# Gate and up of a gated feed-forward layer as one 2x2x2 block product with seven half products, with h kept in DRAM

## The chip, the cores and the metric

One core of a Trainium2 chip. The metric is the device time of one execution in microseconds. Engines: TensorE (PE, with its weight load PEld), VectorE (DVE), ScalarE (ACT), GpSimd (POOL), and SyncE (SP), which issues nearly all DMAs.

## The reference, cut to what matters

One hybrid decoder layer in fp32 on 1024 tokens of width 1024; D_FF = 2816. After the two attention groups and their output projection:

```python
x  = layer_norm(alpha * x + (1 + gate_m) * y, ln1_g, ln1_b)
u2 = x * (1 + scale_f) + shift_f
y2 = (silu(u2 @ w_gate) * (u2 @ w_up)) @ w_down
x  = layer_norm(alpha * x + (1 + gate_f) * y2, ln2_g, ln2_b)
```

Names below: z is the normalized row before ln1_g and ln1_b; x1 = z * ln1_g + ln1_b; h = silu(gate) * up.

## The kernel before, in words

Tokens are in two halves of 512, w_gate and w_up in 22 column blocks f of 128, the width 1024 in 8 slices k of 128. Every fp32 product is three TensorE matmuls (`mm3`): each operand is split into a high part, a cast made by ACT, and a low part, `raw - hi`, made by DVE (`split`, lines 87 and 88), and hi·hi, hi·lo and lo·hi are added in PSUM. One matmul has a 128x128 stationary operand and 512 moving columns. All matmuls of the feed-forward are of this kind, apart from the last row block.

The order within each engine is set by the framework's scheduler, which reorders the program text by its own model; what comes out is fixed before the run and each engine goes through its own list strictly in order. So are the DMAs that SP issues.

- `mixer_units(half, ...)` (lines 829 to 858): per 128 token rows and 512 columns, 12 matmuls `yo`; DVE adds (847), POOL multiplies by the gate (848), DVE adds the residual (849) and takes statistics; with the second column half, mean and 1/sqrt follow on DVE and POOL (`ln_scale`, line 796 on POOL), and ACT writes z (856). Half 0 runs inside the attention, half 1 behind it, in the PSUM tiles b3, w0 and w1.
- `make_u2(rt, mi)` (870 to 886): per slice k, four transposes on TensorE (879), one ACT instruction that applies the modulation (881), a split. It gives u2 of one half of the tokens.
- `mixer_affine` (860 to 866): 16 POOL instructions that turn z into x1; x1 of half 1 goes to DRAM (`x1_d`).
- `ffn_up(us)` (892 to 917): per f, load and split the 128 columns of w_gate and of w_up (two DMAs of 512 KB), 2 x 8 x 3 = 48 matmuls into the two banks of one wide PSUM tile, silu on ACT, product and split on DVE and ACT; h stays in SBUF as hi and lo (the slots `HT`).
- `ffn_down` (919 to 979): per half of the tokens and half of the columns, w_down loaded and split in 11 pieces; 528 matmuls per half of the tokens. At the end of the last quarter four pieces are kept back so that row blocks finish one after the other; the last row block is in two parts of 256 columns. Then `out_norm` (981 to 998).

The text's order is half 0's u2, half 1's mixer units, `ffn_up` of half 0, u2 of half 1, down of half 0, up of half 1, down of half 1. Matmuls of the feed-forward: 2 x 22 x 48 = 2112 for gate and up, 2 x 528 = 1056 for down.

Of the kernel before, what the change touches and what calls it, by code (L numbers as in the profile page):

```python
# [33 lines left out]
def hymba_layer_kernel(  # L34
# [767 lines left out]
    x1_d = dp.tile([S // 2, D], F32, name="x1_d")  # L802
# [23 lines left out]

    ybank = [0]

    def mixer_units(half, rt, yt):
# [3 lines left out]
        def unit(h, q, nb):  # L833
# [6 lines left out]
            tag = ("b3",)[0] if nb == 1 else ('b3', 'w0', 'w1')[ybank[0] % 3]  # L840
# [10 lines left out]
            if h == 1:  # L851
# [37 lines left out]
    HT = (4, 5, 6, 7, 24, 25, 34, 35, 10, 11, 12, 13, 26, 27, 28, 29, 30, 31, 36, 37, 14, 15)  # L889
    fc = [0]  # L890

    def ffn_up(us, between=()):
        ht = []
        between = list(between)
        for f2 in range(NF // 2):
            hh = slot(HT[2 * f2], (2, 512), dt=F32R, name="hh")
            hl = slot(HT[2 * f2 + 1], (2, 512), dt=F32R, name="hl")
            for a in range(2):
                f = 2 * f2 + a
                fs = slice(f * P, (f + 1) * P)  # L900
                ps = wide(f"w{fc[0] % 2}", "gu")
                fc[0] += 1
                for m, w in enumerate((w_gate, w_up)):
                    wh, wl = load_split((NK, P), w[:, fs].rearrange("(k p) n -> p k n", p=P))
                    for k in range(NK):
                        mm3(
                            ps[:, m * 512 : (m + 1) * 512], wh[:, k, :], wl[:, k, :], us[k][0], us[k][1],
                            k == 0, k == NK - 1,
                        )
                sg = tmp512("sg")  # L910
                nc.scalar.activation(sg, ps[:, 0:512], AF.Silu)
                nc.vector.tensor_tensor(sg, ps[:, 512:1024], sg, op=ALU.mult)
                split(hh[:, a, :], hl[:, a, :], sg)
# [165 lines left out]
```

## Time and profile before

| | |
|---|---|
| time, median of 3 runs (lowest to highest) | 1359.32 us (1359.19 to 1360.11) |
| span of the profiled execution | 1358.9 us |
| difference of the span to the median | 0.4 us |
| PE busy | 1319.3 us, 97% |
| DVE / ACT / POOL busy | 625.8 / 482.8 / 246.6 us |
| share of PE in the chain that ended last | 85% |
| matmul records (of all parts) | 6671 |

The profiled execution's own time is not listed apart from its span, so sums are made against the span and 0.4 us is what lies around it. To read the page: the share of busy time is an average over stages; what a change in one stage is worth shows in that stage, by what PE waited for there. A matmul's record lasts longer than the distance to the next one, since matmuls overlap, so the cost of one is the distance of starts.

### The profile page before, as it was taken

What the parts mean: (1) busy time and instruction counts of PE and PEld (TensorE: products, weight loads), DVE (VectorE), ACT (ScalarE), POOL (GpSimd) and SP (SyncE); (2) the same over time, 40 slices, a digit from 0 to 9 for tenths busy, and PEclk for the clock granted to TensorE, in tenths of its full rate; (3) what the DMA queues carried; (4) which work ended last, traced back from release to release, by engine and by line L of the source; (5) the groups of instructions that cost most, each with busy time, mean ns of one, the idle gap of its engine ahead of it and who ended that gap; (6) DMA issues with size and microseconds to landing.
All of it is one profiled execution on the core that took longest, in us unless ns stands there. A gap on an engine that the chain in (4) does not pass through costs nothing.

```text
span 1358.9 us, 16771 instructions
## 1 busy us (share of the span) xinstructions
PE 1319.3 (97%) x6671; PEld 1071.2 (79%) x6671; DVE 625.8 (46%) x927; ACT 482.8 (36%) x812; POOL 246.6 (18%) x244
## 2 busy tenths in 40 slices
PE   5999999999999999988999999999999999999997
PEld 4889987898876666666888888888888888888886
DVE  7665556714353566586433333324373333332244
ACT  3423264423455566443233222522122322222121
POOL 3400114400142454349300000000020000000004
PEclk9999999999999999998999999999999999999999
DMA  9865511110022236314533333332373333332221
GB/s 300 252 221 183 173 48 47 24 32 32 17 64 78 56 108 220 140 47 124 155 93 93 94 93 93 114 119 93 94 216 93 94 96 97 100 95 93 93 94 62
DMA packets 155872, 147.43 MB, mean 108 GB/s; under 512 B 6305, under 2 KB 128267, under 8 KB 155793
## 3 DMA queue, kind: packets, MB, share of 16 engines
q1 hardware_dynamic: 155792, 146.35, 35.0%
q8 instruction: 52, 0.85, 0.3%
q14 instruction: 28, 0.22, 0.1%
HBM read 131.50 MB, written 10.50 MB: 105 GB/s over the span
## 4 chain that ended last, share of the span: by engine, by line
PE 85%; DMA 5%; DVE 5%; ACT 2%; POOL 1%; issue 1%; SPq 0%; POOLq 0%; DVEq 0%; ACTq 0%
PE gu L101 12%; PE gu L100 12%; PE gu L99 12%; PE dn L937 6%; PE dn L938 6%; PE dn L939 6%; DMA wc<-in_w_c_dram 4%; PE pv L756 4%; PE tr L746 3%; PE acc L330 2%; PE acc L331 2%; PE acc L332 2%; PE acc L100 2%; PE acc L101 2%; PE acc L99 2%; PE sc L716 1%
## 5 line engine op out<-in xcount | busy, mean ns | idle before, releaser
L88 DVE TENSOR_TENSOR lo<-raw,hi 128x1024 fp32r<-128x1024 f32 (+1 forms) x161 | 208.1, 1293 | 461.6 <-ACT hi L87 461.6
L87 ACT CAST hi<-raw 128x1024 fp32r<-128x1024 f32 (+1 forms) x161 | 168.9, 1050 | 467.4 <-PE gu L100 272.5
L101 PE MATMUL gu<-u2h,lo 128*128 128x512 f32 x704 | 280.6, 399 | 7.4 <-DVE lo L88 7.4
L100 PE MATMUL gu<-u2l,hi 128*128 128x512 f32 x704 | 279.3, 397 | 2.0 <-DVE u2l L88 2.0
L99 PE MATMUL gu<-u2h,hi 128*128 128x512 f32 x704 | 275.5, 392 | 0.0
L101 PEld LDWEIGHTS gu<-u2h,lo 128*128 128x128 f32 x704 | 132.6, 188 | 36.5 <-DVE lo L88 7.8
L100 PEld LDWEIGHTS gu<-u2l,hi 128*128 128x128 f32 x704 | 132.6, 188 | 34.4 <-DVE u2l L88 2.9
L99 PEld LDWEIGHTS gu<-u2h,hi 128*128 128x128 f32 x704 | 134.6, 191 | 31.2
L796 POOL TENSOR_TENSOR mv<-mv,half_neg 128x1 f32<-128x1 f32 x16 | 21.2, 1327 | 674.3 <-DVE mv L795 674.1
L937 PE MATMUL dn<-hi,hh 128*128 128x512 f32 (+1 forms) x334 | 128.9, 386 | 0.0
L938 PE MATMUL dn<-lo,hh 128*128 128x512 f32 (+1 forms) x334 | 128.4, 385 | 0.0
L939 PE MATMUL dn<-hi,hl 128*128 128x512 f32 (+1 forms) x334 | 127.5, 383 | 0.0
L330 PE MATMUL acc<-hi,uh 128*128 128x264 f32 (+1 forms) x384 | 108.7, 284 | 1.3 <-ACT osb L530 0.8
L331 PE MATMUL acc<-lo,uh 128*128 128x264 f32 (+1 forms) x384 | 108.6, 283 | 0.0
L332 PE MATMUL acc<-hi,ul 128*128 128x264 f32 (+1 forms) x384 | 108.6, 283 | 0.0
L330 PEld LDWEIGHTS acc<-hi,uh 128*128 128x128 f32 x384 | 72.7, 190 | 2.5 <-ACT osb L530 1.0
L331 PEld LDWEIGHTS acc<-lo,uh 128*128 128x128 f32 x384 | 72.8, 190 | 0.8 <-issue 0.5
L939 PEld LDWEIGHTS dn<-hi,hl 128*128 128x128 f32 x334 | 62.6, 188 | 13.7
L937 PEld LDWEIGHTS dn<-hi,hh 128*128 128x128 f32 x334 | 62.7, 188 | 13.4
L721 DVE CUSTOM_DVE_ANT_0 pr<-sc,smask 128x128 f32<-128x128 f32 (+7 forms) x64 | 47.9, 754 | 55.0 <-PE sc L717 31.4
L938 PEld LDWEIGHTS dn<-lo,hh 128*128 128x128 f32 x334 | 62.8, 188 | 12.7
L332 PEld LDWEIGHTS acc<-hi,ul 128*128 128x128 f32 x384 | 72.6, 189 | 0.3
(233 smaller groups left out, 2041.2 us busy)
## 6 DMA issues: line engine op xcount, KB each, us to landing
raw<-in_w_gate_dram SPq DMA_DIRECT2D x44, 512.0 KB, 4.0
raw<-in_w_up_dram SPq DMA_DIRECT2D x44, 512.0 KB, 3.8
raw<-in_w_down_dram SPq DMA_DIRECT2D x44, 512.0 KB, 3.7
wc<-in_w_c_dram SPq DMA_DIRECT2D x32, 512.0 KB, 4.5
wc<-in_w_c_dram SPq DMA_DIRECT2D x32, 256.0 KB, 6.7
raw<-in_w_in_dram SPq DMA_DIRECT2D x15, 512.0 KB, 4.0
raw<-in_w_o_dram SPq DMA_DIRECT2D x12, 512.0 KB, 6.3
xb<-in_x_dram SPq DMA_DIRECT2D x8, 512.0 KB, 5.9
```

Source lines behind the costliest of these rows:

```text
L87: nc.scalar.copy(dst_hi, src)
L88: nc.vector.tensor_tensor(dst_lo, src, dst_hi.bitcast(F32), op=ALU.subtract)
L99: nc.tensor.matmul(ps, lh, rh, start=start, stop=False)
L100: nc.tensor.matmul(ps, lh, rl, start=False, stop=False)
L101: nc.tensor.matmul(ps, ll, rh, start=False, stop=stop)
L330: nc.tensor.matmul(ps, uh[k][:, ts], wh[:, k % 4, :], start=k == 0, stop=False)
L331: nc.tensor.matmul(ps, uh[k][:, ts], wl[:, k % 4, :], start=False, stop=False)
L332: nc.tensor.matmul(ps, ul[k][:, ts], wh[:, k % 4, :], start=False, stop=k == NK - 1)
L756: nc.tensor.matmul(pv[64 * par : 64 * par + 64, 0:256], fv_t(kb)[:, 64 * h : 64 * h + 64], pt[:, par, a * 256 : (a + 1) * 256], start=kb == 0,
L937: nc.tensor.matmul(pq, hh[:, qs], wh[:, c0:c1], start=f == 0, stop=False)
L938: nc.tensor.matmul(pq, hh[:, qs], wl[:, c0:c1], start=False, stop=False)
L939: nc.tensor.matmul(pq, hl[:, qs], wh[:, c0:c1], start=False, stop=f == NF - 1)
```

## The change

Gate and up of all 1024 tokens are taken as one product of 2x2 blocks: the width in two halves (k 0 to 3, k 4 to 7), the tokens in two halves, and gate and up of one block f as the two halves of the columns. Instead of eight half products (each four slices of three matmuls, 12 matmuls) seven are made, by Strassen's identity in the form with few additions. A11 and A12 are the width halves of u2 of half 0 of the tokens, A22 that of half 1; S1 to S4 are sums of the A blocks, B11 and B21 are blocks of w_gate, B22 one of w_up, T1 to T4 sums of the B blocks. Per f: 84 matmuls for both halves of the tokens, 96 before. `first_operands` makes A11 and A12 (A blocks of half 0), `second_operands` A22 and S1 to S4 of the whole run once, `sum_weights` T1 to T4 per f, and `group_parts` the products and the sums of their results (`c11` is a wide PSUM tile with P1 and P2 in one bank and P6 in the other; `x_` and `y_` are single banks).

h of all tokens goes to DRAM per f (`h_d`, 22 stores of 512 KB) and comes back, split again, per pair of f and half of the tokens (`load_h`, 22 loads). `ffn_down` takes one half of the tokens with both column halves in all eight PSUM banks; w_down is loaded 2 x 11 x 2 times as before, and three pieces are kept back at the end of each half. The last row block is 512 columns wide. z instead of x1 goes to DRAM (`z_d`, 8 stores), and the 16 POOL instructions of `mixer_affine` stand in `rows_in`, at the beginning of each `ffn_down`. Half 1's mixer units use the banks b2 and b3. w_gate and w_up are loaded once: 44 DMAs, 88 before. `gaT` and `l2b` share a tag.

```diff
-            tag = ("b3",)[0] if nb == 1 else ('b3', 'w0', 'w1')[ybank[0] % 3]
+            tag = UNIT_BANKS[nb][ybank[0] % len(UNIT_BANKS[nb])]
...
                 nc.scalar.activation(r, r, AF.Identity, bias=mv[:, 3:4], scale=mv[:, 2:3])
+                nc.sync.dma_start(z_d[ts, :], r)
...
+    def second_operands(rt):
...
+        for j in range(NJ):
+            for a in range(2):
+                u2_rows(rt, j + NJ * a, xs[j][:, a, :], f"b{a}")
...
+        for j in range(NJ):
+            t = slot(S_HL[j][4], (2, 512), dt=F32R, name="a22")
+            split(t[:, 0, :], t[:, 1, :], xs[j][:, 1, :])
...
+            nc.vector.tensor_tensor(xs[j][:, 1, :], xs[j][:, 0, :], xs[j][:, 1, :], op=ALU.add)
+            nc.vector.tensor_tensor(xs[j][:, 0, :], af[j][:, 0, :], xs[j][:, 0, :], op=ALU.subtract)
...
+            split(hi, lo, xs[j])
...
+        for j in range(NJ):
+            nc.vector.tensor_tensor(af[j][:, 0, :], xs[j][:, 1, :], af[j][:, 0, :], op=ALU.subtract)
+            nc.vector.tensor_tensor(af[j][:, 1, :], af[j][:, 1, :], af[j][:, 0, :], op=ALU.subtract)
...
+            split(hi, lo, af[j])
...
+    def sum_weights(f, g, u, w):
...
+        nc.vector.tensor_tensor(t12[:, 0], u[:, 0:NJ], g[:, 0:NJ], op=ALU.subtract)
+        nc.vector.tensor_tensor(t12[:, 1], u[:, NJ:NK], t12[:, 0], op=ALU.subtract)
+        nc.vector.tensor_tensor(t34[:, 0], u[:, NJ:NK], u[:, 0:NJ], op=ALU.subtract)
+        nc.vector.tensor_tensor(t34[:, 1], g[:, NJ:NK], t12[:, 1], op=ALU.subtract)
...
+        split(h, l, t12)
...
+        split(h, l, t34)
...
+        split(b[:, 0], b[:, 1], u[:, NJ:NK])
...
+        def p12_a():
+            c11 = st_["c11"] = wide(f"w{par}", "gu")
...
+            product(c11[:, 0:512], w["B11"], opnd["A11"], True)
+            nc.scalar.copy(u, c11[:, 0:512])
+        def p12_b():
+            product(st_["c11"][:, 0:512], w["B21"], opnd["A12"], False)
+        def p6():
+            u, c = st_["u"], st_["c11"]
+            product(c[:, 512:1024], w["T2"], opnd["S2"], True)
+            nc.vector.tensor_tensor(u, c[:, 512:1024], u, op=ALU.add)
...
+        def p43():
...
+            product(x_, w["T4"], opnd["A22"], False)
+            nc.vector.tensor_tensor(g[:, 1, :], x_, u, op=ALU.add)
+            product(y_, w["B22"], opnd["S4"], False)
+            nc.vector.tensor_tensor(h[:, 0, :], y_, u, op=ALU.add)
+            nc.scalar.activation(g[:, 0, :], st_["c11"][:, 0:512], AF.Silu)
+            nc.scalar.activation(g[:, 1, :], g[:, 1, :], AF.Silu)
+            nc.vector.tensor_tensor(h, g, h, op=ALU.mult)
+            nc.sync.dma_start(h_d[f // 2][f % 2, :, :], h.rearrange("p a n -> p (a n)"))
...
+        def load_h(i, hi, lo):
+            raw = slot(HRAW[pc[0] % 2], (2, 512), name="hr")
+            nc.sync.dma_start(raw, h_d[i][:, :, half * 512 : (half + 1) * 512].rearrange("f p n -> p f n"))
+            split(hi, lo, raw)
...
+    first_operands(xa)
     for f in mixer_units(1, xb, yb):
-        f(2)
+        f(3)
+    second_operands(xb)
...
+            p12_a()
+            p6()
+            p12_b()
+        p7()
+        p5()
+        mid()
+        p43()
...
+    rows = {0: rows_in(0), 1: None}
...
+    ffn_down(0)
+    rows[1] = rows_in(1)
+    ffn_down(1)
```

PE behind the last `yo` matmuls of half 1's mixer units, before (`gu` with `u2h`, `u2l` are gate and up of half 0):

```order
L844 MATMUL yo_5557<-hi_5507,ofh_4837 128x512
L845 MATMUL yo_5557<-lo_5508,ofh_4837 128x512
L846 MATMUL yo_5557<-hi_5507,ofl_4838 128x512
L99 MATMUL gu_5609<-u2h_5335,hi_5612 128x512
L100 MATMUL gu_5609<-u2l_5336,hi_5612 128x512
```

and of the change (`u2p` are transposes of z, `r_5346` the last row block of half 1, `a1h` and `a1l` A11 and A12):

```order
L846 MATMUL yo_5586<-lo_5511,ofh_4848 128x512
L847 MATMUL yo_5586<-hi_5510,ofl_4849 128x512
L873 MATMUL u2p_5614<-ident,r_5334 128x128 [waits PE_49,Activation_49]
L873 MATMUL u2p_5620<-ident,r_5334 128x128 [waits DVE_49,PE_49]
...
L873 MATMUL u2p_5614<-ident,r_5346 128x128 [waits Activation_49]
L873 MATMUL u2p_5620<-ident,r_5346 128x128 [waits DVE_49]
...
L967 MATMUL gu_5755<-a1h_5363,hi_5726 128x512 [waits Activation_49]
L967 MATMUL gu_5755<-a1l_5364,hi_5726 128x512
```

The 32 transposes of half 1 now stand between the last `yo` matmul and the first product; before, products of half 0 followed at once.

DVE in the change, from the first row of A22 to the first sum of product results (`x2` is u2 of half 1, `af` that of half 0, `s31l` and `s24l` low parts of S3 and S1, S2 and S4; 38 rows from the first to the last but one of these):

```order
L88 TENSOR_TENSOR a22_969_5662<-x2_957_5610,a22_969_5662 128x512 [waits Activation_49]
L910 TENSOR_TENSOR x2_957_5610<-x2_957_5610 128x512 [waits DVE_49]
L911 TENSOR_TENSOR x2_957_5610<-af_909_5350,x2_957_5610 128x512 [waits DVE_49]
...
L918 TENSOR_TENSOR af_909_5350<-x2_957_5610,af_909_5350 128x512 [waits DVE_49]
...
L88 TENSOR_TENSOR s24l_988_5719<-af_924_5401,s24h_987_5718 128x1024 [waits DMAHW0_49,PE_49,Activation_49]
L992 TENSOR_TENSOR hf_1005_5756<-gu_1004_5755,hf_1005_5756 128x512 [waits PE_49]
```

All of them are in one queue, ahead of the first sum of results; before, no such rows exist.

PE in the middle of the change's gate and up, where P6 of one block ends and P2 begins (`gu` is the wide tile, `gy` the bank of P5), and the DVE row that reads P6's result:

```order
L967 MATMUL gu_6243<-s24h_5718,hi_6232 128x512
L967 MATMUL gu_6243<-s24l_5719,hi_6232 128x512
L967 MATMUL gu_6243<-s24h_5718,lo_6233 128x512
L967 MATMUL gy_6296<-s31l_5695,hi_6232 128x512
L967 MATMUL gy_6296<-s31h_5694,lo_6233 128x512
L967 MATMUL gu_6243<-a1h_5363,hi_6222 128x512 [waits DVE_49]
```

```order
L992 TENSOR_TENSOR hf_1065_6244<-gu_1064_6243,hf_1065_6244 128x512 [waits DMAHW1_49,PE_49,Activation_49]
```

Behind the last P6 matmul two matmuls of P5 follow, and then P2, which waits for the DVE row. Before, a block's 48 matmuls had no such wait among them.

## Rows read from the trace of the kernel before

**Rows 1.** Windows by stage: length, then busy us (instructions) of PE, PEld, DVE, ACT, POOL; granted clock, DMA share, GB/s

```profile
600.30:616.30 16.00, 6.59 (x30) 4.45 (x28) 16.00 (x16) 5.70 (x8) 14.11 (x8) 0.78 0.11 33
616.30:1350.80 734.50, 734.48 (x3242) 599.94 (x3242) 279.38 (x316) 203.46 (x244) 59.91 (x28) 1.00 0.34 104
1350.80:1358.90 8.10, 0.00 (x0) 0.00 (x0) 4.36 (x8) 0.00 (x0) 3.50 (x3) 0.66 0.35 129
```

**Rows 2.** A window that holds only gate, up and down matmuls

```profile
973.00:1226.00 253.00, 253.00 (x1092) 205.67 (x1091) 101.02 (x120) 70.97 (x88) 8.36 (x4) 1.00 0.37 111
```

**Rows 3.** PE timeline behind the mixer units: start, length, instruction [idle before <-releaser]

```profile
599.91 0.40 PE L846 MATMUL yo<-hi,ofl 128*128 128x512 f32 x1
...
602.00 0.60 PE L879 MATMUL u2p<-ident,r 128*128 128x128 f32 x4
...
605.15 0.51 PE L100 MATMUL gu<-u2l,hi 128*128 128x512 f32 x1 [0.69 <-DVE u2l L88]
605.50 0.39 PE L101 MATMUL gu<-u2h,lo 128*128 128x512 f32 x1
...
607.94 0.50 PE L100 MATMUL gu<-u2l,hi 128*128 128x512 f32 x1 [1.35 <-DVE u2l L88]
...
616.26 0.80 PE L101 MATMUL gu<-u2h,lo 128*128 128x512 f32 x1 [7.37 <-DVE lo L88]
...
619.71 0.39 PE L100 MATMUL gu<-u2l,hi 128*128 128x512 f32 x1
```

**Rows 4.** DVE timeline, a mixer unit and its normalization

```profile
562.39 0.20 DVE L794 BATCH_NORM_AGGREGATE mv<-bs 128x2 f32<-128x12 f32 x1
...
563.23 0.69 DVE L847 TENSOR_TENSOR yp<-yo,yp 128x512 f32<-128x512 f32 x1
...
565.33 0.69 DVE L849 SCALAR_TENSOR_TENSOR r<-r,yp 128x512 f32<-128x512 f32 x1 [1.23 <-POOL yp L848]
```

**Rows 5.** POOL timeline, one product of a mixer unit

```profile
564.00 1.29 POOL L848 TENSOR_TENSOR yp<-yp,raw 128x512 f32<-128x512 f32 x1
```

**Rows 6.** POOL groups by form, 600 to 700 us: busy us, mean ns | idle before

```profile
L864 POOL TENSOR_TENSOR r<-r,l1b 128x1024 f32<-128x1024 f32 x8 | 24.0, 3017 | 0.0
...
L796 POOL TENSOR_TENSOR mv<-mv,half_neg 128x1 f32<-128x1 f32 x4 | 3.7, 932 | 0.0
```

**Rows 7.** ACT timeline behind the mixer units

```profile
605.19 0.78 ACT L881 ACTIVATE uf<-u2p,mcol 128x512 f32<-128x512 f32 x1 [1.79 <-DVE u2l L88]
606.00 0.62 ACT L87 CAST u2h<-uf 128x512 fp32r<-128x512 f32 x1
615.11 1.24 ACT L856 ACTIVATE r<-r,mv 128x1024 f32<-128x1024 f32 x1 [8.49 <-DVE mv L853]
```

**Rows 8.** DVE timeline: a low part whose end releases PE

```profile
615.00 1.21 DVE L88 TENSOR_TENSOR lo<-raw,hi 128x1024 fp32r<-128x1024 f32 x1
```

**Rows 9.** DVE timeline: pairs of instructions in direct succession

```profile
597.73 0.68 DVE L88 TENSOR_TENSOR u2l<-uf,u2h 128x512 fp32r<-128x512 f32 x1
598.33 0.68 DVE L847 TENSOR_TENSOR yp<-yo,yp 128x512 f32<-128x512 f32 x1
...
1051.24 1.23 DVE L88 TENSOR_TENSOR lo<-raw,hi 128x1024 fp32r<-128x1024 f32 x1 [4.32 <-ACT hi L87]
1052.39 0.68 DVE L912 TENSOR_TENSOR sg<-gu,sg 128x512 f32<-128x512 f32 x1
```

**Rows 10.** The page's DMA issues, loads of w_gate: count, KB each, us to landing

```profile
raw<-in_w_gate_dram SPq DMA_DIRECT2D x44, 512.0 KB, 4.0
```

**Rows 11.** Timeline: a last matmul of a row block, and the DVE instruction that reads it

```profile
1344.64 0.39 PE L939 MATMUL dn<-wdh,hl 128*128 128x512 f32 x1
...
1345.07 0.69 DVE L945 TENSOR_TENSOR tmp<-dn,gf 128x512 f32<-128x512 f32 x1 [1.67 <-PE dn L939]
```

**Rows 12.** DVE timeline: a low part made while POOL runs 128x1024 instructions

```profile
608.40 2.79 DVE L88 TENSOR_TENSOR lo<-raw,hi 128x1024 fp32r<-128x1024 f32 x1
```

**Rows 13.** DVE timeline behind the last matmul

```profile
1350.81 0.42 DVE L945 TENSOR_TENSOR tmp<-dn,gf 128x256 f32<-128x256 f32 x1 [0.72 <-PE dn L939]
```

More of the change, by code (lines that the diff above doesn't have):

```diff
@@ L825, in mixer_weights @@
         ]
+    UNIT_BANKS = {1: ("b3",), 2: ("b3", "w0", "w1"), 3: ("b2", "b3")}
     ybank = [0]
@@ L889, in hymba_layer_kernel @@
[L889 to L893, printed above, removed]
-        between = list(between)
-        for f2 in range(NF // 2):
-            hh = slot(HT[2 * f2], (2, 512), dt=F32R, name="hh")
-            hl = slot(HT[2 * f2 + 1], (2, 512), dt=F32R, name="hl")
-            for a in range(2):
[L899 to L913, printed above, removed]
-                ht.append((hh[:, a, :], hl[:, a, :]))
@@ new lines, in hymba_layer_kernel, with first_operands @@
+    af = []
+    def first_operands(rt):
+        ops = []
+        for j in range(NJ):
+            t = slot(A1_F[j], (2, 512), name="af")
+            for a in range(2):
+                u2_rows(rt, j + NJ * a, t[:, a, :], f"b{a}")
+            hi = slot(A1_HL[j][0], (2, 512), dt=F32R, name="a1h")
+            lo = slot(A1_HL[j][1], (2, 512), dt=F32R, name="a1l")
+            split(hi, lo, t)
+            af.append(t)
+            ops.append((hi, lo))
+        for a, name in ((0, "A11"), (1, "A12")):
+            opnd[name] = [(h[:, a, :], l[:, a, :]) for h, l in ops]
@@ new lines, in load_block, with first_weights @@
+    def load_block(f):
+        fs = slice(f * P, (f + 1) * P)
+        g = wtile("raw", (NK, P), F32)
+        nc.sync.dma_start(g, w_gate[:, fs].rearrange("(k p) n -> p k n", p=P))
+        u = wtile("raw", (NK, P), F32)
+        nc.sync.dma_start(u, w_up[:, fs].rearrange("(k p) n -> p k n", p=P))
+        return g, u
+    def first_weights(g, w, slots=None):
+        if slots is None:
+            gh, gl = wtile("hi", (2, NJ, P), F32R), wtile("lo", (2, NJ, P), F32R)
+        else:
+            gh, gl = [slot(i, (2, NJ, P), dt=F32R, name="b1") for i in slots]
+        split(gh.rearrange("p a k n -> p (a k) n"), gl.rearrange("p a k n -> p (a k) n"), g)
+        w["B11"], w["B21"] = (gh[:, 0], gl[:, 0]), (gh[:, 1], gl[:, 1])
@@ new lines, in hymba_layer_kernel, with rows_in @@
+    HG = (14, 15)
+    ROWS = ((0, 1, 2, 3), (10, 11, 12, 13))
+    HRAW, HHI, HLO = (34, 35), (8, 16, 18), (9, 17, 19)
+    NKEEP = 3
+    KEPT = ((26, 27, 28, 29, 30, 31), (20, 21, 22, 23, 36, 37), (32, 33, 24, 25, 4, 5))
+    pc = [0]
+    def rows_in(half):
+        rt = []
+        for q in range(4):
+            t = 4 * half + q
+            r = slot(ROWS[half][q], name="r2")
+            nc.sync.dma_start(r, z_d[t * P : (t + 1) * P, :])
+            nc.gpsimd.tensor_tensor(r, r, l1g, op=ALU.mult)
+            nc.gpsimd.tensor_tensor(r, r, l1b, op=ALU.add)
+            rt.append(r)
+        return rt
@@ new lines, in ffn_down @@
+        kept = []
+        for n in range(NKEEP):
+            i = NF // 2 - NKEEP + n
+            ks = KEPT[n]
+            h = (slot(ks[0], (2, 512), dt=F32R, name="kh"), slot(ks[1], (2, 512), dt=F32R, name="kl"))
+            load_h(i, *h)
+            pc[0] += 1
+            w = []
+            for d in range(2):
+                raw = wtile("raw", (2, 512), F32)
+                nc.sync.dma_start(raw, w_src(i, d))
+                hi = slot(ks[2 + 2 * d], (2, 512), dt=F32R, name="kwh")
+                lo = slot(ks[3 + 2 * d], (2, 512), dt=F32R, name="kwl")
+                split(hi, lo, raw)
+                w.append((hi, lo))
+            kept.append((i, h, w))
@@ L946, in evac @@
+        rt = rows[half]
+        for q in range(4):
+            bs = new_bs()
+            for d in range(2):
+                hs = slice(d * 512, (d + 1) * 512)
+                for i, h, w in kept:
+                    mms(i, q, d, h, w[d])
+                tmp = tmp512("tmp")
+                nc.vector.tensor_tensor(tmp, acc[2 * q + d], gf[:, hs], op=ALU.mult)
                 nc.vector.scalar_tensor_tensor(
-                    rt[q][:, cs], rt[q][:, cs], ALPHA, tmp, op0=ALU.mult, op1=ALU.add
+                    rt[q][:, hs], rt[q][:, hs], ALPHA, tmp, op0=ALU.mult, op1=ALU.add
```

224 lines of the change are left out of this document (125 added, 99 removed).

## Prediction

> **What bounds the kernel now.** I read the windows by stage first. From 616.30 us to 1350.80 us PE is busy 734.48 of 734.50 us at a granted clock of 1.00, the level of 2.4 GHz, while DVE has 279.38 and ACT 203.46 [rows 1]: the reader is to see that in this stage nothing is faster unless PE has fewer matmuls, and that a new wait of PE is paid in full. The price of a matmul is the distance of starts: in a window that holds nothing but gate, up and down, 1092 of them take 253.00 us, 0.2317 us each [rows 2]; the single record lasts 0.39 us [rows 3] because matmuls overlap. Then I read PE's timeline where the mixer units end. The last `yo` matmul ends at 599.91 + 0.40 = 600.3 us, products of half 0 follow, and the stretch of 16 us has three waits: 0.69, 1.35 and 7.37 us [rows 3]. After the long one the clock has fallen: from 616.26 to 619.71 us eight matmuls start at 0.43 us each, the level of 1.2 GHz, which costs 8 x 0.20 = 1.6 us. After the short ones it has not: 605.15 to 605.50 us is 0.35, 0.12 over the usual distance, and the next record has 0.39 us again [rows 3].
>
> The feed-forward as a whole: from 600.3 to the end of PE at 1350.8 us [rows 1] are 750.5 us. 2112 + 1056 = 3168 matmuls at 0.2317 are 734.0, so 16.5 us are lost: 9.4 in waits, 1.6 by the clock, and 36 transposes at 0.60 / 4 = 0.15 us [rows 3], 5.4 us.
>
> **The change, part by part.** *Fewer matmuls.* 22 blocks x 12 fewer = 264, x 0.2317 = **61.2 us** less. All of them lie on PE's path. Down keeps its 1056.
>
> *Half 1's units end at about the same time.* The transposes of half 0 that stood behind 600.3 now stand ahead of it: 4 x 0.15 = 0.6 us later.
>
> *The way into the first block.* Before, half 0's products covered the normalization of half 1. Now PE's list has all 32 transposes of half 1 ahead of the first product, so the last unit's tail is bare: 0.69 (sum) [rows 4], 1.29 on POOL [rows 5], 0.69 (residual) and as much for the statistics, three column instructions of 0.20 at most [rows 4], the power on POOL 0.93 [rows 6], z on ACT 1.24 [rows 7]: 6.1 us, and nine hand-offs between engines at 0.05 (a low part ends at 616.21, PE starts at 616.26 [rows 3, 8]) make 6.6. The last transpose, two modulations of 0.78 and a cast of 0.62 us [rows 7], with hand-offs, are 2.5. Then DVE has 38 instructions in one list between the first A22 and the last low part of S2 and S4: 12 of 128x1024 and 26 of 128x512. In succession these take 0.60 us (597.73 to 598.33) to 0.68, and 1.15 to 1.23 for the long form [rows 9]: 29.4 to 32.4, and I take 31, since some of them wait for casts. ACT beside it has 15 casts of 0.62 and 12 of at most 1.24 us [rows 7], 24 us, so DVE sets the pace. Behind the last low part stand 2 matmuls of P6 and the 12 of P2 of block 1: 3.3 us. By then 84 products are done (60 of block 0, 24 of block 1). The stretch is 6.6 + 2.5 + 31 + 3.3 = **43.4 us** from the last `yo` matmul, of which the products are worth 19.5; 24 us are lost. Bounds: 21 with DVE at its fastest and some covered hand-offs; 32 if DVE also waits for the first weights, whose loads stand on SP's list behind the last store of z, and take 4.0 us to land [rows 10], or for ACT.
>
> *The middle, blocks 2 to 21.* PE's list has, at the end of P6, two matmuls of P5, then P2, which waits for DVE's reading of P6's result; P6 and P2 are halves of one wide tile. A DVE instruction of this form starts 0.43 us after the start of the last matmul (1344.64 to 1345.07) and takes 0.69 [rows 11]; with 0.05 for the hand-off P2 may start at 1.17. Its place in the list comes at 3 x 0.2317 = 0.70. The wait of 0.47 and the slow restart of 0.12 [rows 3] make 0.58 us per block, x 20 = **11.6 us**. Bounds: 0.3 (6 us) if the first matmul hides part of it, 1.0 (20 us) if DVE is in the middle of another 0.69 us instruction. The rest of a block is covered: DVE's ten short and four long instructions are 10 x 0.69 + 4 x 1.23 = 11.8 us, of 84 x 0.2317 = 19.5; ACT's casts, copy and silus are at most 5 x 0.78 + 3 x 1.24 = 7.6 [rows 7]. One pair of loads per 19.5 us at 4.0 [rows 10] is less than one pair per 11.1 before. The store of h is half a block's traffic and nothing on PE waits for it before its slot is used two blocks later.
>
> *Down.* The matmuls of one pair of f are 48 x 0.2317 = 11.1 us. DVE splits three pieces for them, one more than before per 48 matmuls, 3 x 1.23 = 3.7 us: covered. The 16 POOL instructions of `rows_in`, 3.0 us each [rows 6], lie beside about four pairs. A split beside such instructions took 2.79 instead of 1.23 us [rows 12]; 3 x 2.79 = 8.4 is still under 11.1, so I take 0. By the rule in the Trainium skill, "SBUF — State Buffer", section "Who interferes with whom", a DVE instruction with two SBUF inputs and a GpSimd one that reads SBUF lock each other out for their whole length, and by that the sum would be some 7 us higher (E below). The trace agrees that they disturb each other, 2.79 us, and not that it is for a whole 3.0 us. The last rows of half 0 and the first of half 1 share PSUM banks in order, with one 0.69 us read each, while 7 other banks are at work: 0.
>
> *The end.* The last row block has 512 columns instead of two times 256; three DVE instructions of 0.42 [rows 13] become 0.69 [rows 11]: 8.1 [rows 1] + 0.8 = 8.9 us.
>
> **Sum.** 600.3 + 0.6 + 43.4 + (1848 - 84 + 1056 = 2820) x 0.2317 = 653.3, + 11.6 + 8.9 = 1318.1 us of span; 0.4 lie between span and median, so **1318.5 us**, 40.8 less than 1359.3. Of the 61.2 us, 24 - 16.5 = 7.5 are given back by the bare preparation in place of the old losses, 11.6 by P2's wait, and 1.4 by the early transposes and the end.
>
> **Rivals.**
>
> *B, the preparation and P2's wait are covered* (PE loses no more than the 16.5 us it lost before, and P2 comes no later than its place). For it: DVE has much spare time in the windows, 279 of 735 us [rows 1]. Against it: PE's list, which has no product to put ahead of the transposes. 1318.5 - 11.6 - (24 - 16.5) = **1299 us**.
>
> *C, the clock falls at each P2.* If twenty waits each cost what the 7.37 us wait cost, eight matmuls at 0.43 us, that is 20 x 1.6 = 32 more: **1351 us**. Against it: after 0.69 us and after 1.35 us of waiting records kept 0.39 to 0.40 us [rows 3]; mine is 0.47.
>
> *D, slower than before.* DVE goes through its list in order; ahead of the read of P6's result stand sums and low parts of the next block's weights, which wait for loads and casts. Before, DVE stood 4.32 us for such a cast, which itself waited for PE to leave a buffer [rows 9]. If that delay sits ahead of the read, P2 waits as long, once per block. It decides from 41 / 20 = 2 us above my 0.58, some 2.6 us per block; at 3 us the time is 1318.5 - 11.6 + 60 = **1367 us**. Against it: DVE's 11.8 us of work in 19.5, and the row right ahead of the read is the product of the block before, whose inputs are some 12 matmuls older.
>
> *E, POOL locks DVE out at the beginning of each down.* Each of three splits would wait for one POOL instruction: 3 x (1.23 + 3.0) = 12.7 against 11.1 us of matmuls, 1.6 us per pair, over 48 / 11.1 = 4.3 pairs: 7 us, **1325 us**. That the 2.79 us record [rows 12] shows only half of such a wait speaks against it.
>
> *That the change does not do what it says*: PE's list has the 264 matmuls less, so only the measurement of no change at all would show it, about 1359 us.
>
> **How the numbers follow.** The forecast has 0.70, E 0.09, B 0.08, C 0.07, D 0.05, no change 0.01. The time is that of the forecast. Its bounds: the middle at 6 instead of 11.6 and the preparation at 21 instead of 24 give 1310; 20 and 32 give 1335. E lies inside. A measurement of this kernel tells 0.2%, 2.7 us, from no change, and I widen both ends by that: **1307 to 1338 us**; outside lie B, C and D, 0.20. Faster by over 0.2%: all but D and no change, 0.93 with a little of C's upper part taken off; within 0.2%: 0.02; slower: 0.05.
>
> **What would show each step.** In the changed kernel's windows PE must show 264 matmul records fewer and a distance of 0.23 us in the middle. Behind the last `yo` record PE should be idle for some 9 us, then run products with waits on DVE's `s31l`, `s24l` and T low parts for some 31 us; if that stretch, to the first full block, is near 27 us, B is right there. In each middle block the first P2 matmul should show some 0.5 us of idle time released by DVE line 992, and the records behind it 0.39 us; records of 0.63 us there, with a granted clock under 1.00 in the middle windows, are C; waits of 2 us or more, D. In the first pairs of down, PE idle time released by low parts of `raw` is E. Wrong would be any share of PE under 97% between the first full block and the last matmul, a wait of PE on a DMA of h, or a gap between the two halves of down.

## The result and the profile after

The change takes 1324.24 us (median of 4 runs, 1323.76 to 1327.68) where the kernel before takes 1359.26 us: 35.0 us less, a ratio of 0.9739 (95% interval 0.9720 to 0.9757). Timed again later, beside the last of the experiments, it had 1324.89 us against 1363.09, 0.9719 (0.9699 to 0.9739). The forecast was 1318.5 us, 40.8 less, with a range of 1307 to 1338.

First the windows of the changed kernel by stage: up to the last `yo` matmul's end, the way into the first blocks, the rest of gate and up, down, and the end (columns as in [rows 1]):

```profile
0.00:602.13 602.13, 576.95 (x3405) 465.04 (x3405) 328.08 (x591) 274.52 (x561) 170.67 (x209) 1.00 0.37 114
602.13:647.41 45.28, 32.05 (x117) 23.53 (x117) 37.07 (x61) 28.76 (x34) 4.71 (x6) 0.70 0.38 116
647.41:1069.20 421.79, 414.72 (x1769) 331.40 (x1768) 243.51 (x296) 117.50 (x149) 6.68 (x3) 1.00 0.29 93
1069.20:1313.68 244.48, 242.22 (x1053) 197.08 (x1052) 149.23 (x140) 66.47 (x68) 66.37 (x27) 1.00 0.46 153
1313.68:1322.50 8.82, 0.00 (x0) 0.00 (x0) 5.04 (x8) 0.00 (x0) 1.45 (x1) 0.73 0.25 92
```

PE is still the bound, but no longer without gaps: in the middle it lacks 7.1 us of 421.8 and in down 2.3 of 244.5, where before it lacked nothing [rows 1]. The clock is 1.00 in both, and 0.70 on the way in. PE's waits from 590 us on (what waited, for whom: sum us, times, longest us):

```profile
PE gu L967 <- DVE hf L992: 7.1, 19, 0.4
PE u2p L873 <- ACT r L857: 6.3, 4, 4.1
PE gu L967 <- DVE lo L88: 2.9, 1, 2.9
PE gu L967 <- ACT hi L87: 2.6, 1, 2.6
PE dn L1063 <- ACT hi L87: 1.4, 1, 1.4
PE yo L845 <- DVE yp L848: 1.4, 2, 0.7
PE u2p L873 <- ACT x L874: 1.4, 3, 0.7
PE dn L1063 <- DVE tmp L1105: 0.9, 1, 0.9
```

The first row is P2's wait, in 19 of the 20 blocks 2 to 21; rows two to four and seven are the way in, row six is ahead of it, rows five and eight are in down, at the end of its first half. No row names a low part of S1 to S4. PE's timeline on the way in, to be laid beside [rows 3]:

```profile
601.73 0.40 PE L847 MATMUL yo<-hi,ofl 128*128 128x512 f32 x1
606.19 0.69 PE L873 MATMUL u2p<-ident,r 128*128 128x128 f32 x2 [4.06 <-ACT r L857]
...
617.65 1.11 PE L873 MATMUL u2p<-ident,r 128*128 128x128 f32 x4 [0.50 <-ACT x L874]
621.38 0.80 PE L967 MATMUL gu<-a1h,hi 128*128 128x512 f32 x1 [2.62 <-ACT hi L87]
621.98 0.63 PE L967 MATMUL gu<-a1l,hi 128*128 128x512 f32 x1
625.51 0.79 PE L967 MATMUL gu<-a1h,lo 128*128 128x512 f32 x1 [2.91 <-DVE lo L88]
...
631.77 0.39 PE L967 MATMUL gu<-a1h,lo 128*128 128x512 f32 x1
```

From 602.1 to 625.5 us PE has transposes and two matmuls; then the clock is low and matmuls start every 0.43 us until 630.8. PE has no wait from 625.51 to 647.41, where 84 matmuls of the products are done. The middle, one block apart:

```profile
817.83 0.40 PE L967 MATMUL gy<-s31h,lo 128*128 128x512 f32 x1
818.60 0.50 PE L967 MATMUL gu<-a1h,hi 128*128 128x512 f32 x1 [0.37 <-DVE hf L992]
818.94 0.40 PE L967 MATMUL gu<-a1l,hi 128*128 128x512 f32 x1
...
838.72 0.50 PE L967 MATMUL gu<-a1h,hi 128*128 128x512 f32 x1 [0.37 <-DVE hf L992]
```

The period is 838.72 - 818.60 = 20.12 us against 84 x 0.2317 = 19.46: 0.65 us per block for a listed wait of 0.37, since the first matmul behind a wait is slow too. The matmuls behind have 0.39 to 0.40 us.

### The profile page after: what moved, and what is told of

Its sections match the earlier page's. It is cut to its first block, busy times and chain, and to the rows that moved or that the text cites. A ratio compares the mean times of both kernels' runs of the same rounds, so it can differ in the third digit from the quotient of the medians.

```text
span 1322.5 us, 16317 instructions
## 1 busy us (share of the span) xinstructions
PE 1266.0 (96%) x6341; PEld 1017.0 (77%) x6341; DVE 762.9 (58%) x1093; ACT 487.2 (37%) x812; POOL 249.9 (19%) x244
## 4 chain that ended last, share of the span: by engine, by line
PE 67%; issue 12%; DMA 7%; DVE 7%; ACT 3%; POOL 2%; SPq 1%; POOLq 0%; DVEq 0%; ACTq 0%
PE gu L967 11%; PE gy L967 6%; PE gx L967 6%; PE dn L1063 5%; PE dn L1064 5%; PE dn L1065 5%; PE pv L756 4%; DMA wc<-in_w_c_dram 4%; PE tr L746 3%; PE acc L330 2%; PE acc L331 2%; PE acc L332 2%; PE acc L100 2%; PE acc L101 2%; PE acc L99 2%
## 5 line engine op out<-in xcount | busy, mean ns | idle before, releaser
L87 ACT CAST hi<-raw 128x1024 fp32r<-128x1024 f32 (+1 forms) x86 | 90.0, 1049 | 289.0 <-PE gy L967 151.7
L88 DVE TENSOR_TENSOR lo<-raw,hi 128x1024 fp32r<-128x1024 f32 (+1 forms) x86 | 122.3, 1424 | 107.6 <-ACT hi L87 107.4
L1064 PE MATMUL dn<-lo,hh 128*128 128x512 f32 x256 | 100.5, 392 | 0.0
L1065 PE MATMUL dn<-hi,hl 128*128 128x512 f32 x256 | 100.2, 392 | 0.0
L1063 PE MATMUL dn<-hi,hh 128*128 128x512 f32 x256 | 93.8, 393 | 1.4 <-ACT hi L87 1.4
L967 PE MATMUL gu<-a1h,hi 128*128 128x512 f32 x168 | 69.6, 414 | 9.7 <-DVE hf L992 7.1
L87 ACT CAST hi<-t 128x1024 fp32r<-128x1024 f32 x44 | 46.1, 1050 | 85.6 <-PE gu L967 43.8
L88 DVE TENSOR_TENSOR lo<-t,hi 128x1024 fp32r<-128x1024 f32 x44 | 53.8, 1225 | 30.2 <-ACT hi L87 29.8
L967 PE MATMUL gu<-a1h,lo 128*128 128x512 f32 x168 | 67.7, 403 | 2.9 <-DVE lo L88 2.9
L967 PE MATMUL gu<-a1l,hi 128*128 128x512 f32 x168 | 67.4, 401 | 0.0
L756 PE MATMUL pv<-pt,fv 128*64 128x256 f32 x320 | 61.5, 396 | 0.5 <-DVE ofl L88 0.5
```

What stands on the lines that cost most here:

```text
L87: nc.scalar.copy(dst_hi, src)
L88: nc.vector.tensor_tensor(dst_lo, src, dst_hi.bitcast(F32), op=ALU.subtract)
L756: nc.tensor.matmul(pv[64 * par : 64 * par + 64, 0:256], fv_t(kb)[:, 64 * h : 64 * h + 64], pt[:, par, a * 256 : (a + 1) * 256], start=kb == 0,
L967: nc.tensor.matmul(ps, x, y, start=start and j == 0 and i == 0, stop=j == NJ - 1 and i == 2, skip_group_check=not start,)
L1063: nc.tensor.matmul(ps, hh, wh, start=i == 0 and a == 0, stop=False)
L1064: nc.tensor.matmul(ps, hh, wl, start=False, stop=False)
```

## The experiments

All ratios are to the kernel before in the same runs. The change's own ratio was 0.9739 in one set of runs and 0.9719 in another, so a difference of 0.002 says nothing. Of the seven products, P1 is B11 with A11, P2 B21 with A12, P3 B22 with S4, P4 T4 with A22, P5 T1 with S1, P6 T2 with S2 and P7 T3 with S3. Two theories were to be tested, each against a rival: that P2's place in the list, and nothing else, costs some 13 us in the middle; and that on the way in it is DVE's list that sets the end (L), not PE's late start (W).

**e1: P5 behind P6**, so that 12 matmuls instead of 2 stand between P6 and P2.

```diff
+            with tc.issue_after(st_["l6"].ins):
-            product(y_, w["T1"], opnd["S1"], True)
+                product(y_, w["T1"], opnd["S1"], True)
```

> Edit: P5 is issued behind P6, so that 12 matmuls of P5 instead of 2 stand between P6 and P2. My theory: the middle loses 0.65 us per block at P2 (block period 20.12 us against 84 x 0.2317 = 19.46) because DVE's read of P6's result is not covered; with 2.8 us of cover the wait is gone: 13 us less than the 1324.2 us of the change, 1311 us. Rival: DVE's list is in order and the wait only moves, to P4 behind it (which waits for the next sum on DVE) or to P7: 1322 to 1324 us, and PE waits of about 0.4 us per block on another DVE row.

Measured: 1315.44 us, 0.9652 (0.9635 to 0.9668). The row of P2's wait is gone, and from 660 to 1050 us PE waits for nothing at all, where it was busy 383.30 us in the change:

```profile
660.00:1050.00 390.00, 390.00 (x1688) 317.88 (x1687) 222.89 (x277) 107.31 (x139) 0.27 (x1) 1.00 0.28 89
```

A block takes 731.63 - 712.17 = 19.46 us from one P6 to the next, 84 x 0.2317, so the theory holds for the middle. But the time fell by some 9 to 12 us only (0.0067 to 0.0087 by the change's two ratios). By the two traces, 1.4 us go back on the way in (46.7 us from the last `yo` matmul to block 0's P4, for 45.3), and some 4.5 in down (249.7 us from the last product to the last matmul, for 245.2 in the change with the four down matmuls counted that stand ahead there). PE's timeline shows most of the latter at the beginning of down:

```profile
1060.51 0.50 PE L1066 MATMUL dn<-lo,hh 128*128 128x512 f32 x1 [1.86 <-DVE lo L88]
...
1062.59 0.63 PE L1066 MATMUL dn<-lo,hh 128*128 128x512 f32 x1
1063.01 0.63 PE L1067 MATMUL dn<-hi,hl 128*128 128x512 f32 x1
```

A wait of 1.86 us for a low part that the change does not have, and a little behind it seven matmuls 0.43 us apart, 1.4 us more, with a granted clock of 0.84 from 1055 to 1065 us; most of the rest, 0.9 us, are longer waits at the end of the first half of down. The rival was right that something comes back, and wrong on where; e10 looks at it.

**e1b: P6 behind all of P5**, nothing between P6 and P2.

```diff
             p12_a()
-            p6()
-            p12_b()
-        p7()
-        p5()
+            p7()
+            p5()
+            p6()
+            p12_b()
...
+            with tc.issue_after(st_["l5"].ins) if "l5" in st_ else nullcontext():
+                product(c[:, 512:1024], w["T2"], opnd["S2"], True)
```

> Edit: P6 is issued behind all of P5, so that nothing stands between P6 and P2. My theory of the wait (0.43 us to DVE's start, 0.69 us of DVE, 0.05 us to PE, less one place of 0.23 us): it grows from 0.37 to 0.83-0.94 us, 0.46 us more in 20 blocks: 1333.5 us, and the matmuls behind it keep 0.39 us. Rival (the clock): a wait of that length in every block lets the clock fall, eight matmuls at 0.43 us or 1.6 us more each: 1366 us, with a granted clock under 1.00 in the middle.

Measured: 1337.86 us, 0.9816 (0.9802 to 0.9831): 0.0077 to 0.0097 over the change by the two ratios of the change, 10.5 to 13 us, for 9.3 expected. By the traces gate and up are 9.9 us longer, which is the theory's part, and down is 3.8 us longer, which it did not have. PE's timeline in the middle:

```profile
821.17 0.40 PE L967 MATMUL gu<-s24h,lo 128*128 128x512 f32 x1
822.41 0.50 PE L967 MATMUL gu<-a1h,hi 128*128 128x512 f32 x1 [0.84 <-DVE hf L994]
822.75 0.39 PE L967 MATMUL gu<-a1l,hi 128*128 128x512 f32 x1
```

The wait grew from 0.37 to 0.84, by the 0.46 us of the two matmuls that no longer cover it: P2 starts 1.24 us after P6's last matmul started, where I had worked out 1.17. And the clock stays: 0.39 us behind the wait, 1.00 from 700 to 900 us. Twenty waits of 0.84 us, 20 us apart, don't lower it; the rival of the clock falls.

**e2: block 0's P1 and P2 ahead of the transposes.**

```diff
-    second_operands(xb)
     ws = [{}, {}]
     raws = load_block(0)
     first_weights(raws[0], ws[0])
+    gs = [group_parts(0, ws[0])]
+    gs[0][0]()
+    gs[0][1]()
+    second_operands(xb)
     sum_weights(0, *raws, ws[0])
```

> Edit: P1 and P2 of block 0 (24 matmuls, 5.6 us) and the first weights' load and split stand ahead of the transposes of half 1. Theory L (DVE's list of operand sums sets the end of the way in; in the change its last low part is ready only 1.3 us before PE comes to it): 1 to 3 us less, 1321 to 1323 us, and PE then waits for low parts of S2 and S4. Rival theory W (PE is late because the first weights come late, at 625.5 us, and because the clock has fallen by then; DVE's list has slack): all of the 5.6 us and the 2.9 us of slow matmuls come back, 1316 us.

Measured: 1329.29 us, 0.9754 (0.9740 to 0.9769), no better than the change. 24 matmuls of the products were done by 609 us, and PE then waited longer:

```profile
617.38 0.69 PE L873 MATMUL u2p<-ident,r 128*128 128x128 f32 x2 [8.61 <-ACT r L857]
```

DVE's and POOL's timelines, and ACT's, say why:

```profile
599.37 1.78 DVE L950 TENSOR_TENSOR t<-raw 128x512 f32<-128x512 f32 x1
...
609.23 1.20 DVE L88 TENSOR_TENSOR lo<-t,hi 128x1024 fp32r<-128x1024 f32 x1
610.35 0.68 DVE L848 TENSOR_TENSOR yp<-yo,yp 128x512 f32<-128x512 f32 x1
```

```profile
598.93 1.67 POOL L849 TENSOR_TENSOR yp<-yp,raw 128x512 f32<-128x512 f32 x1 [4.68 <-DVE yp L848]
```

```profile
616.09 4.64 ACT L857 ACTIVATE r<-r,mv 128x1024 f32<-128x1024 f32 x4 [7.96 <-DVE mv L854]
```

The scheduler moved block 0's weight sums ahead of the normalization on DVE's list; the last unit's `yp` (848) came at 610.35 us though its matmuls had ended at 606.0, and the first rows of z were with PE 11.4 us behind the last mixer matmul instead of 4.1. Since DVE's list grew along with PE's cover, e2 alone does not decide between L and W. The rows also show how DVE and POOL meet: a DVE instruction of 0.68 us took 1.78 and ended at 601.15, 0.55 us after POOL's at 600.60.

**e5: e2 with block 0's weight sums held behind the normalization**; **e9: e5 without the 16 operand sums** (S1 to S4 are made of unsummed operands, so four of the seven products are of other data).

```diff
-    sum_weights(0, *raws, ws[0])
+    with tc.issue_after(ln_last[0].ins):
+        sum_weights(0, *raws, ws[0])
```

```diff
-            nc.vector.tensor_tensor(xs[j][:, 1, :], xs[j][:, 0, :], xs[j][:, 1, :], op=ALU.add)
-            nc.vector.tensor_tensor(xs[j][:, 0, :], af[j][:, 0, :], xs[j][:, 0, :], op=ALU.subtract)
...
-            nc.vector.tensor_tensor(af[j][:, 0, :], xs[j][:, 1, :], af[j][:, 0, :], op=ALU.subtract)
-            nc.vector.tensor_tensor(af[j][:, 1, :], af[j][:, 1, :], af[j][:, 0, :], op=ALU.subtract)
```

> Edit: as e2, but the sums of block 0's weights stay behind the last DVE instruction of half 1's normalization. In e2 they went ahead of it on DVE's list and z came 11.4 us after the last mixer matmul instead of 4.1. Theory L (DVE's list sets the way in): the normalization is as short as in the change, the weight sums fill the 4.3 us in which DVE stood idle behind it, one low part of 1.2 us is out of the list; the last low part comes 4 to 5 us earlier: ratio to before 0.970 to 0.971 against 0.9739 of the change and 0.9754 of e2. Rival W (e2 showed that PE's cover is worth nothing): no better than the change, 0.974.

> Edit: e5 without the 16 DVE sums that make S1 to S4 (the operands are split unsummed, so these four products are of other data). Theory L: DVE's list between the normalization and block 0 is 16 x 0.6 = 9.6 us shorter and the time falls until PE's own work (36 transposes and 60 matmuls behind them) is what is left: 5 to 8 us under e5. Rival W: nothing changes.

Measured: e5 1323.97 us, 0.9718 (0.9694 to 0.9742), e9 1317.60 us, 0.9681 (0.9656 to 0.9705). e5 is better than e2, but hardly than the change. Its normalization is short again (the last rows' transposes start 8.5 us behind the last mixer matmul, as they do in the change with 8.4), yet the last low part comes at 644.89 + 1.22 = 646.1 us, not 4 to 5 us earlier but 3.2 later than in the change (641.68 + 1.22 = 642.9):

```profile
644.89 1.22 DVE L88 TENSOR_TENSOR s24l<-af,s24h 128x1024 fp32r<-128x1024 f32 x1
```

DVE is busy all the way from 613.0, but for 1.1 us. Two things took the gain: the products that went ahead of the last `yo` matmuls made these end 3.8 us later, and with them all of DVE's list; and four sums and a low part of block 1's weights, 3.5 us, went ahead of the last low parts. Here W falls: the products stand ahead and the normalization is short, and of the 8 us that W would give back hardly anything comes (the last product starts at 1068.3 us, in the change at 1069.0), since DVE's list ends later. e9 takes 9.6 us out of the same list and is 6.4 us faster than e5 by the medians, 5.0 by the ratios, within what L expected. Together: L holds, and a shorter wait of PE is worth nothing here unless DVE's list becomes shorter or starts earlier.

**e7: eight of the 16 operand sums on POOL.**

```diff
-            nc.vector.tensor_tensor(xs[j][:, 1, :], xs[j][:, 0, :], xs[j][:, 1, :], op=ALU.add)
+            (nc.gpsimd if j in (1, 2) else nc.vector).tensor_tensor(xs[j][:, 1, :], xs[j][:, 0, :], xs[j][:, 1, :], op=ALU.add)
...
```

> Edit: of the change, the 8 operand sums of two of the four slices are on POOL instead of DVE. Theory without a lock between the engines: DVE's list is 8 x 0.6 = 4.8 us shorter and the change some 3 to 5 us faster, 0.970 to 0.972. Rival, the lock seen in e2 (a DVE instruction of 0.68 us took 1.78 us, up to 0.55 us behind the end of the POOL instruction beside it): each POOL sum of some 1.3 us stops DVE for its whole length, longer than the 0.6 us that it saves; 3 to 6 us slower, 0.976 to 0.978.

Measured: 1330.87 us, 0.9770 (0.9748 to 0.9793), 0.0031 to 0.0051 over the change, 4 to 7 us, as the lock says. DVE's timeline:

```profile
618.47 2.29 DVE L88 TENSOR_TENSOR s31l<-x,s31h 128x1024 fp32r<-128x1024 f32 x1
620.68 2.28 DVE L88 TENSOR_TENSOR s24l<-af,s24h 128x1024 fp32r<-128x1024 f32 x1
622.89 1.76 DVE L88 TENSOR_TENSOR a<-x,a 128x512 fp32r<-128x512 f32 x1
```

Low parts of 1.22 us took 2.28, those of 0.69 us 1.76: 1.07 us more each. Eight DVE instructions are longer like this, one per POOL instruction (one of them by 0.95 us), so an instruction that POOL takes over costs DVE more (1.07) than it saves (0.6). PE's wait for the first weights' low part, 2.91 us in the change, is 9.08 us here, and the stretch to block 0's P4 is 6.2 us longer (51.46 for 45.28): a longer list on DVE is paid by PE, which is once more L.

**e6: e5 and e1 together; e11: e6 with block 1's weight sums also held back**, behind the last low part of S2 and S4.

```diff
-    sum_weights(1, *raws, ws[1])
+    with tc.issue_after(ln_last[0].ins):
+        sum_weights(1, *raws, ws[1])
```

> Edit: e5 and e1 together. The two losses lie in different stages, so they should add: 0.9652 of e1 and 4 to 5 us: ratio to before 0.961 to 0.962, some 1309 us where before is 1362. If the shorter way in only moves the loss to the first blocks: 0.965.

> Edit: e6, and the sums of block 1's weights stay behind the last low part of S2 and S4 on DVE's list (in e5 four of these sums and a low part, 3.5 us, stood ahead of it). Theory L: the last low part comes some 3 us earlier and block 0 with it: ratio to before 0.962 to 0.963, against 0.965 of e6. Rival: block 1 then waits for its own weights and gives it back: 0.965.

Measured: e6 1313.84 us, 0.9651 (0.9634 to 0.9668), not told from e1, so e5's way in did not add to e1, as its second theory said; e11 **1312.12 us, 0.9629** (0.9611 to 0.9647), the fastest of those that leave nothing out, 12.8 us under the change in the same runs (1324.89), though told from e1 only by the trace: the last low part comes at 637.19 + 2.43 = 639.6 us, and gate and up end at 1051.4 us, against 1053.7 of e6 and 1056.2 of e1. DVE's row of the last two low parts in e11:

```profile
637.19 2.43 DVE L924 TENSOR_TENSOR s24l<-af,s24h 128x1024 fp32r<-128x1024 f32 x2
```

**e4: eight half products instead of seven**, all else as in the change.

```diff
-            product(c[:, 512:1024], w["T2"], opnd["S2"], True)
...
+        for t, pg, pu in ((0, c[:, 0:512], c[:, 512:1024]), (1, x_, y_)):
+            product(pg, w["B11"], opnd[f"A{t + 1}1"], True)
+            product(pg, w["B21"], opnd[f"A{t + 1}2"], False)
+            nc.scalar.activation(g[:, t, :], pg, AF.Silu)
+            product(pu, w["B12"], opnd[f"A{t + 1}1"], True)
+            product(pu, w["B22"], opnd[f"A{t + 1}2"], False)
+            nc.vector.tensor_tensor(h[:, t, :], pu, g[:, t, :], op=ALU.mult)
```

> Edit: eight half products instead of seven (gate and up straight, no sums of operands or weights, no sums of results), all else as in the change: both halves of the tokens per block, h through DRAM, down over both column halves. My theory: 264 matmuls more, 61.2 us; no P2 wait, 13 us less; a shorter list on DVE ahead of the first products, some 7 us less: 1324.2 + 61.2 - 13 - 7 = 1365 us, that is some 5 us over the kernel before, which is the bare normalization and the wider end, and h through DRAM costs nothing. Rival: h's way through DRAM or the larger down have a hidden cost that the saved matmuls paid for: 1370 us and more.

Measured: 1372.29 us, 1.0076 (1.0057 to 1.0094): 9.7 us over before in the same runs, and 0.0337 to 0.0357 over the change by its two ratios, 46 to 49 us. By the traces gate and up, from the last `yo` matmul to the last product, take 47.1 us more than in the change without its four early down matmuls. The arithmetic of the identity, 61.2 less some 13 for P2, is 48.2. In its middle PE is busy all of the time:

```profile
700.00:900.00 200.00, 200.00 (x864) 162.59 (x863) 34.52 (x36) 28.75 (x36) 0.00 (x0) 1.00 0.24 74
```

864 matmuls in 200 us with h going to DRAM: the store costs PE nothing there. I had expected 1365 and the rival 1370 and more, which is what was measured; but the trace puts the excess on the way in (`yo` ends at 601.7, the first product waits for its high part until 622.03 us, and some 12 matmuls then start 0.43 us apart), not on h. Gate and up take 513.5 us for 2112 matmuls, 489.4 at 0.2317, so 24.1 are lost there; down takes 246.2 for 244.7, 1.5 lost. That is 25.6 us where the kernel before lost 16.4 in the whole; the units before end 1.4 us later and the end is 0.7 longer, and with the 9.2 more that are lost this makes the 11.3 us by which the two traces differ. At most the 1.5 us of down are left for a hidden cost of h's way.

**e10: e6 without the 16 POOL instructions of the rows** (ln1_g and ln1_b are not applied in the residual).

```diff
-            nc.gpsimd.tensor_tensor(r, r, l1g, op=ALU.mult)
-            nc.gpsimd.tensor_tensor(r, r, l1b, op=ALU.add)
```

> Edit: e6 without the 16 POOL instructions that apply ln1_g and ln1_b to the rows (that part of the output is left out). In e1 and e6 PE waits some 5 us at the beginning of down for high and low parts, 2.3 us in the change, while DVE's low parts alternate with these POOL instructions at 3.35 us each. If POOL is the cause, 2 to 4 us under e6, and DVE's low parts in down at 1.22 us; if the waits are those of a pipeline that starts with the first h (store, load, split), no difference.

Measured: 1310.91 us, 0.9630 (0.9604 to 0.9656). By time alone that is not told from e6; by the traces it is: gate and up end alike (1053.6 and 1053.7 us), and from there to the last matmul it takes 245.9 us against 249.2. DVE's groups from 1045 to 1120 us, of e6 and then of e10 (busy us, mean ns | idle before):

```profile
L88 DVE TENSOR_TENSOR hl<-hr,hh 128x1024 fp32r<-128x1024 f32 x8 | 22.9, 2872 | 0.0
```

```profile
L88 DVE TENSOR_TENSOR hl<-hr,hh 128x1024 fp32r<-128x1024 f32 x8 | 9.7, 1222 | 1.4 <-ACT hh L87 1.4
```

The wait of 1.9 us for a low part, which e1, e6 and e11 have at the beginning of down, is gone, so POOL is its cause. The other waits that the expectation put at the beginning of down are not there but at the end of its first half, at 1138 to 1170 us, and they stay: 2.9 us in e6, 1.9 and 1.2 in e10, 1.4 and 0.9 in the change, 2.0 and 0.3 in e12. So of the 3.3 us between e6 and e10 some 2 are POOL's; the rest is at that later place, where two traces of one kernel differ too. The change has the same POOL instructions without the wait: they start 3.1 us before its first down matmul (1062.5 and 1065.6 us), in e6 6.3 us before (1047.7 and 1054.0). That this is why it has no wait was not tested.

**e12: the change again**, for the second ratio above.

> The change itself on the chip of these runs, for a comparison without a change of chip: 0.974 of before, P2 waits of 0.37 us in 19 or 20 blocks.

P2's wait is the same in it, 7.1 us in 19 blocks. The last `yo` matmul ends at 603.15 us in it and at 602.13 in the first trace of the change, so that point varies by 1 us between traces of one kernel.

## Why the prediction was right, and where it was off

**Fewer matmuls.** Right: PE's records fell by 330, the 264 and the 66 that the last row block had in its second part, and e4 shows that the identity is worth some 47 us here, P2's wait paid.

**The middle.** Right in mechanism, place and nearly in size: 0.58 us per block worked out, 0.65 measured, in 19 blocks instead of 20, 12.4 instead of 11.6 us. The wait is that of the list, as e1 and e1b show by removing and doubling it. Rivals C and D fall: clock 1.00, and no wait over 0.4 us in the middle.

**The way in.** 43.4 us forecast, 45.28 measured, where [rows 1] have the 16.0 us of before. Three parts. The normalization was put at 9.1 us from the last matmul to the first low part of A22; it took 613.16 - 602.13 = 11.0. The step that failed is the first: I let DVE add the last unit's sum 0.05 us after its matmuls, but DVE was still at the residuals and statistics of the units before, and got to it 2.0 us late:

```profile
604.15 0.64 DVE L848 TENSOR_TENSOR yp<-yo,yp 128x512 f32<-128x512 f32 x1
...
613.16 0.69 DVE L88 TENSOR_TENSOR a<-x,a 128x512 fp32r<-128x512 f32 x1 [4.25 <-ACT a L87]
...
624.24 1.22 DVE L88 TENSOR_TENSOR lo<-raw,hi 128x1024 fp32r<-128x1024 f32 x1
...
641.68 1.22 DVE L88 TENSOR_TENSOR s24l<-af,s24h 128x1024 fp32r<-128x1024 f32 x1
```

The 38 instructions took 642.90 - 613.16 = 29.7 us for 31, with no idle time among them. And PE came to the last low part not at once but late, 4.5 us to the end of the 84 matmuls instead of 3.3.

The last part is more than a size: the predicted sign, PE's waits on low parts of S1 to S4 for some 31 us, did not come. DVE's list holds PE at another row. The low part of the first weights (624.24) stands in the middle of it, and PE waits for that until 625.51; the 82 matmuls behind it then take 21.9 us without a wait, 82 x 0.2317 = 19.0 and 2.9 for the low clock, and end the stretch. PE comes to the last low part 1.3 us after it is done. That the sum of the other path, the whole list and 14 matmuls, came so near is partly luck: in the change the two paths end within 1.3 us of each other. With PE's products ahead (e5) the whole list is the bound, as I had it; e5 gains nothing, e9 and e11 gain by a shorter or better ordered list, and e7 loses by a longer one.

**The units before.** Put at 0.6 us for moved transposes; the last `yo` ended at 602.13 instead of 600.9. The term that I left out is PE's wait for DVE's `yp` in these units, 1.4 us in the list of waits, with two PSUM banks instead of three; the kernel before has no wait of PE from 540 to 601 us. No run tested the number of banks, and traces of one kernel differ by 1 us at this point (e12).

**Down.** Put at 0, it lost 2.3 us in waits. Two things are to be told apart.

The first is rival E, POOL's lock. The rule of the Trainium skill ("SBUF — State Buffer", "Who interferes with whom") was weighed wrongly: I read the 2.79 us record [rows 12] as half a lock. The runs agree with the Trainium skill here: DVE stands until POOL's instruction ends, as e2 and e7 show. What was wrong in rival E is its price. DVE and POOL alternate,

```profile
1080.11 3.42 DVE L88 TENSOR_TENSOR lo<-raw,hi 128x1024 fp32r<-128x1024 f32 x1
1083.46 3.41 DVE L88 TENSOR_TENSOR hl<-hr,hh 128x1024 fp32r<-128x1024 f32 x1
1086.79 3.42 DVE L88 TENSOR_TENSOR lo<-raw,hi 128x1024 fp32r<-128x1024 f32 x1
```

every 3.35 us, not every 1.23 + 3.0: POOL's 3.0 us [rows 6] already hold its own waiting for DVE. Three per pair of f are 10.05 us, just under the 11.1 of PE. POOL's 16 instructions last from 1062.5 to 1116.0 us, and PE has no wait in that time. So in the change the lock costs PE nothing, as the 0 for it said.

What failed is the rest of the 0, for the end of the first half. The two waits lie there, one for a high part of w_down and one for DVE's reading of a finished row block:

```profile
1152.15 1.19 PE L1063 MATMUL dn<-hi,hh 128*128 128x512 f32 x4 [1.40 <-ACT hi L87]
...
1168.82 0.50 PE L1063 MATMUL dn<-kwh,kh 128*128 128x512 f32 x1 [0.85 <-DVE tmp L1105]
```

ACT's rows show what held the first one back: on ACT's list that cast stands behind the cast of a kept piece, which waited 4.38 us for its load.

```profile
1150.11 1.05 ACT L87 CAST kwh<-raw 128x1024 fp32r<-128x1024 f32 x1 [4.38 <-DMA raw<-in_w_down_dram]
1151.06 1.04 ACT L87 CAST hi<-raw 128x1024 fp32r<-128x1024 f32 x1
```

DVE's reading at 1168.08 us, in turn, comes right behind three low parts of w_down and h. I had counted the PSUM banks and their reads of 0.69 us at this place, and not the lists of ACT and DVE, which cast and split the next pieces at the same time. No run changed this place, so the cause is read from the traces and not shown by an experiment.

**The sum.** Base and time around the span: I took 0.4 us from the median and the span. Each run now lists both, and they lie 1.7 us apart in either kernel (1360.49 and 1358.8 of before, 1324.17 and 1322.5 of the change): by that distance the profiled execution of before, span 1358.9, was itself some 1.3 us slower than the median. With 1.2 for the units, 1.9 for the way in, 1.4 for middle and down together (2.3 of waits in down and 0.8 at P2, less 1.7 because matmuls start closer than 0.2317, 437 in 100 us from 1200 us on), -0.1 for the end and 1.3 for the base, that is the 5.7 us by which the forecast was short. That the waits of down and the closer starts nearly cancel is luck. B's 1299 us was out of reach: even e11, with P2 covered and DVE's list in better order, has 0.9629 of before, 1309 us by that ratio.

## What to carry to other kernels

When a change buys matmuls with sums, write down the list of the engine that makes the sums, where it starts and what PE needs of it last; work that is moved ahead to fill PE's gap helps only if that list does not grow or start later by it, and the scheduler put the wrong half of it first here. Look at the places where one stage hands over to the next, too: the waits of down that the forecast lacked lie where the pieces kept back are loaded, cast and split, at the end of the first half. When two products share a PSUM tile and one's result is read in between, count the matmuls that stand behind the first: 1.24 us from the last matmul's start to the next use is five places here, and reordering them took 13 us out of the middle. POOL was no help here for work whose operands both lie in SBUF while DVE did such work at the same time: e7 lost by it.

## What was not expected of the hardware

Two engines that take turns at SBUF show times that contain each other: POOL's 128x1024 instruction is 3.0 to 3.35 us beside DVE, and a DVE instruction's excess beside POOL's 128x512 one was 1.07 us, so neither record may be added to the other. And the clock held at 1.00 with a PE wait of 0.84 us in every 20.6 us, while behind the idle stretches of the way in twelve matmuls in a row started 0.43 to 0.45 us apart. One wait of the same length did both: behind 1.86 us at the beginning of down seven matmuls started 0.43 us apart in e1, and behind 1.87 us at the same place in e6 none did.
